# A convolution's buffer taken late, its norm run as a line of stages, and new counts of three engines' time in the order of a conformer layer

## The chip, the cores and the metric

The kernel runs on one core of one Trainium2 chip. The metric is the device time of one execution in microseconds (us); lower is better. The engines are named as in the profile: PE is TensorE (matmuls; PEld its weight loads), DVE is VectorE, ACT is ScalarE, POOL is GpSimd, and SP (SyncE) issues most of the DMAs.

## The reference

One inference step of a one-layer streaming encoder for a prompt of 2048 frames and a sample of 64, D_MODEL 1024, in float32. The two mixers work on the same normalised input, and the feed-forward part follows. Cut to what matters:

```python
h = rms_norm(x, p['norm1_g']) * (1 + sc1) + sh1
z = h @ p['w_in']
glu_a, glu_b, q, k, v, g_conv, g_attn = jnp.split(z, offs, axis=-1)

u = glu_a * jax.nn.sigmoid(glu_b)                       # (T, 512)
conv_out, conv_state = conv_module(u, conv_hist, ...)

q = rms_norm(q.reshape(B, T, 8, 64), p['q_norm_g'])
k = rms_norm(k.reshape(B, T, 8, 64), p['k_norm_g'])
o = attend(q, k, v, p['rel_bias'])                      # own chunk of 64 and the 8 before
attn_out = o @ p['w_attn_out']

merged = jax.nn.sigmoid(g_conv) * conv_out + jax.nn.sigmoid(g_attn) * attn_out
x = x + gt1 * (merged @ p['w_o'])
h2 = rms_norm(x, p['norm2_g']) * (1 + sc2) + sh2
gate, up = jnp.split(h2 @ p['w_ffn_in'], 2, axis=-1)
x = x + gt2 * ((jax.nn.silu(gate) * up) @ p['w_ffn_out'])

def conv_module(u, hist, w_dw, b_dw, ln_g, ln_b, w_out):
    ext = jnp.concatenate([hist, u], axis=1)
    y = depthwise_conv(ext, w_dw)                       # 31 taps, causal, 512 channels
    y = jax.nn.silu(layer_norm(y + b_dw, ln_g, ln_b))   # norm over the 512 channels
    return y @ w_out, ext[:, -30:]
```

The time is mostly matmuls with float32 operands that are split into a high and a low part (`hi` by ACT, `lo = x - hi` by DVE or POOL) and multiplied in three products.

## The kernel before

**Two phases.** The first phase goes over four blocks of tokens (576, then three of 512, the sample's 64 in the first): for each block the stages `q`, `0`, `k`, `1`, `v`, `2`, `3`, `g` of `ORDER`. `q`, `k`, `v` are projections; the stages 0 to 3 each make 128 channels (a column tile `ct`) of the convolution's input `u` by `glu`; `g` makes the 16 gate column tiles of both mixers. Beside these matmuls run the attention of the block, the taps of the convolution and its norm. The second phase takes three blocks of 576, 768 and 768 tokens: it merges both mixers (`merge`), applies `w_o`, and does the feed-forward part. Between the phases the first phase's pools are closed and the second's are opened in the same SBUF, so that a tile of the second phase waits for the last reader of what lay in its place.

**The order.** PE executes in the order in which the program emits its instructions. What accompanies the projections is written as generators in `Lane`s. A `Stream` holds a count of nanoseconds for each of `pe`, `dve`, `act` and `pool`; every instruction that goes through a `Meter` adds an estimate in `Stream.add` to its engine's count, beginning no earlier than PE's count. `stream.when("dve")` is DVE's count less 200 ns (`LAG`), and a generator that yields it is stepped on only when PE's count has come that far. Every 500 ns of PE's count `tick` looks at the lanes in the order norm_lane, work (q and k rows), attn, tail, conv. A lane may have a room: `conv` is stepped, up to four times a tick, only while DVE's count is less than 2000 ns ahead of PE's; attention may go to 3000 for DVE and 4000 for ACT. A yielded function parks the generator until it answers true. `drain` steps whatever is left, due or not. The estimates before: ACT 220 + 0.83 n ns for n elements of a partition, POOL 60 + 2.25 n (260 n for a power), DVE 75 + 1.04 n, or 0.75 n for `tensor_scalar` and copies and 8.3 n for a reciprocal. The other engines' order is made from the program by a scheduler; only PE's is as written.

**The convolution.** `convolve(u, y, ct, b)` multiplies the first of the 31 taps into `y[:, ct]` and adds 30 more, one DVE instruction each, `y <- u, wd, y`, with a yield after each. `u` has three buffers, `y` one for all four column tiles of a block. In stage 0 of each block the loop drains `conv` and `tail` and then takes a new `y`.

**The norm.** After stage 3 `conv_norm` goes to the lane `tail` (in block 0 twice, for the sample's 64 columns and the prompt's 512). It is parked until no convolution is open; then it sums the four column tiles on POOL (`s <- y`), adds up the channels by a matmul with ones (`pm`), subtracts the mean (DVE), squares (ACT), sums (POOL), a second matmul with ones, root (ACT), reciprocal (DVE, in four pieces), four products `y <- y, s` (POOL). Then for each column tile in turn: tanh (ACT, `ln <- y, lnh`), scale and product (DVE), high part (ACT, `part_h <- ln`), low part (DVE, `part_l <- ln, part_h`), and the store of both to `c_d` by SP, with a yield between each. `part_h` and `part_l` come from `parts()`, two buffers each, which the q and k rows (`store_kq`, from `kn`) and the attention's results (`finish_head`, from `o_p`) use as well.

**The end of the first phase.** At gate tile 10 of block 3 (`SIDE_G`) the loop drains `work` and `conv` and begins to load the second phase's first operands; after the last gate tile it drains `attn`, `conv` and `tail`.

Of the kernel before, what the change touches and what calls it, by code (L numbers as in the profile page):

```python
# [8 lines left out]
F32 = mybir.dt.float32  # L9
F32R = mybir.dt.float32r  # L10
AF = mybir.ActivationFunctionType
# [5 lines left out]
P = 128  # L17
# [7 lines left out]
TAPS = 31  # L25
# [149 lines left out]
class Stream:  # L175
# [7 lines left out]
    def add(self, name, op, n, args, kw):  # L183
        if name == "pe":
            x = args[1]
            if op == "transpose" or kw.get("is_transpose"):
                ns = 128 / 1.2
            elif x.dtype == F32:
                ns = max(n, 64) / (2.4 if "tile_position" in kw else 0.6)
            else:  # L190
                ns = (n if n >= 256 else 512) / 2.4
        elif name == "act":
            ns = 220 + 0.83 * n
        elif name == "pool":
            ns = 260.0 * n if ALU.pow in args else 60 + 2.25 * n
        else:
            fast = op in ("tensor_scalar", "tensor_copy")
            ns = 75 + n * (8.3 if op == "reciprocal" else 0.75 if fast else 1.04)
        self.load[name] = max(self.load[name], self.load["pe"]) + ns

    def full(self, room):
# [421 lines left out]
def streaming_layer(ctx: ExitStack, tc: tile.TileContext, I, O):  # L623
# [647 lines left out]
        W.done()  # L1271
        return u

    def convolve(u, y, ct, b):
        w = UW if b == 0 else HIST + QB
        n = w - HIST
        states = [(cs_s, HIST + SMP)] if b == 0 else [(cs_p, w)] if b == len(PBLOCKS) - 1 else []
# [2 lines left out]
        for rows_, e in states:  # L1280
# [4 lines left out]
            stream.at(stream.when("dve"), lambda s=s, rows_=rows_: nc.sync.dma_start(rows_[:, ct * P : (ct + 1) * P], s))  # L1285
            yield
        gps.tensor_copy(hist[:, ct], u[:, w - HIST : w])
        dve.tensor_scalar(y[:, ct, :n], u[:, :n], wd[:, ct, 0:1], bdw[:, ct : ct + 1], ALU.mult, ALU.add)
        for k in range(1, TAPS):
            with tc.issue_after(ahead_of_taps[-1]) if ahead_of_taps else nullcontext():  # L1290
                dve.scalar_tensor_tensor(
                    y[:, ct, :n], u[:, k : k + n], wd[:, ct, k : k + 1], y[:, ct, :n], ALU.mult, ALU.add
                )
            yield

    def conv_norm(y, c0, n, t0):
        yv = y[:, :, c0 : c0 + n]
        yield lambda: not conv.gens
        s = wk.tile([P, 512], F32, tag="ln_s", bufs=1)

        def total():
# [3 lines left out]

        gps.tensor_tensor(s[:, :n], yv[:, 0], yv[:, 1], ALU.add)
        for ct in (2, 3):
            gps.tensor_tensor(s[:, :n], s[:, :n], yv[:, ct], ALU.add)
        yield stream.when("pool") + PE_LAG
        pm = total()  # L1310
# [17 lines left out]
            dve.reciprocal(s[:, c:e], s[:, c:e])  # L1328
            yield
        yield stream.when("dve")  # L1330
        done = []
        for ct in range(4):
            gps.tensor_tensor(yv[:, ct], yv[:, ct], s[:, :n], ALU.mult)
            done.append(stream.when("pool"))
        for ct in range(4):
            yield done[ct]
            tmp = temp("ln")
            act.activation(tmp[:, :n], yv[:, ct], AF.Tanh, bias=lnh[:, 4 + ct : 5 + ct], scale=lnh[:, ct : ct + 1])
            yield stream.when("act")
            dve.tensor_scalar(yv[:, ct], yv[:, ct], lng[:, ct : ct + 1], lnb[:, ct : ct + 1], ALU.mult, ALU.add)  # L1340
            dve.scalar_tensor_tensor(tmp[:, :n], tmp[:, :n], 1.0, yv[:, ct], ALU.add, ALU.mult)
            yield stream.when("dve")
            hi, lo = parts()
            act.activation(hi[:, :n], tmp[:, :n], AF.Copy)
            yield stream.when("act")
            name = low(hi[:, :n], lo[:, :n], tmp[:, :n], n, TT_LESS)

            def store(ct=ct, hi=hi, lo=lo):
                for l, a in enumerate((hi, lo)):
                    nc.sync.dma_start(c_d[l, ct, :, t0 : t0 + n], a[:, :n].bitcast(F32))  # L1350

            stream.at(stream.when(name), store)

    def gates(b, free):

# [292 lines left out]
    for b, stage in ORDER:  # L1648
# [21 lines left out]
        elif stage == "g":  # L1670
            spare["open"] = b >= 2
            for g in gates(b, free):
# [7 lines left out]
                        norm_lane.add(gen)  # L1680
                if g == SIDE_G and b == len(PBLOCKS) - 1:
                    work.drain()
                    conv.drain()
                    while spare["heads"] and now["scored"] < spare["heads"][-1]:
                        attn.push()
                    stream.flush()
                    side.close()
                    wc = ctx.enter_context(tc.tile_pool(name="wc", bufs=1, side="right"))
                    cs = tile_chunks(*CBLOCKS[0])[0]
                    src = load_mixed(*cs, 0)  # L1690
                    first_gates = gate_columns(*cs, 0)
            norms = ahead
        else:
            if b == 0 and stage == 1:
                bias_rows()
            if stage == 0:
                conv.drain()
                tail.drain()
                y = wk.tile([P, 4, YW], F32, tag="y", name="y")
            conv.add(convolve(glu(b, stage), y, stage, b))  # L1700
            if stage == 3:
                if b == 0:
                    tail.add(conv_norm(y, 0, SMP, 0))
                    tail.add(conv_norm(y, SMP + HIST, QB, SMP))
                else:
                    tail.add(conv_norm(y, 0, QB, lo))
        for _ in range(MODS.get((b, stage), 0)):
            next(mods)
    next(mods)
    attn.drain()  # L1710
    conv.drain()
    tail.drain()
    stream.flush()
    side.close()
# [667 lines left out]
```

## Time and profile before

| what | before |
|---|---|
| median of 3 runs | 2942.79 us (2941.39 to 2945.29) |
| the profiled execution: its own time | 2941.67 us |
| its span, first to last instruction | 2939.5 us |
| busy: PE, DVE, ACT, POOL | 98%, 70%, 46%, 40% |
| mean granted clock of PE | 0.997 |
| HBM read and written | 476.53 and 148.54 MB |

The span is that of one profiled execution. A busy PE is not one at its peak: matmuls are pipelined and their ends modelled. "A <- B: x, n, m" in the list of waits means that A waited x us for B in total, n times, at most m us. "L105" is the line of `Meter` through which nearly all instructions are issued, so groups are told apart by the names of their tiles: out <- in. Phase one lasts until about 1163 us of the span; the four blocks' stage `q` ends at about 67, 341, 642 and 916 us.

### The profile page before, as it was taken

The page shows a single profiled execution, that of the slowest core. Times are in us where ns is not written, and L with a number is a line of the kernel's source. Part 1 is how long each engine was busy: PE and PEld are TensorE (multiplying, and loading weights), DVE is VectorE, ACT ScalarE, POOL GpSimd, SP SyncE. Part 2 cuts the span into 40 slices and gives each one's busy share as a digit, 9 for nine tenths or more (in the row PEclk, how much of TensorE's full clock was granted, in tenths as well). Part 3 has the DMA queues.
Part 4 walks back from the last instruction along what each step waited for, and adds up shares of the span by engine and source line. Part 5 has one row for each costly group of instructions (what it writes and reads, how often), then busy time and mean ns, then how long its engine had stood idle before and what let it go on. Part 6 is the DMA issues. An engine that isn't in the chain of part 4 may idle for free.

```text
span 2939.5 us, 44832 instructions
## 1 busy us (share of the span) xinstructions
PE 2889.3 (98%) x16193; PEld 2587.5 (88%) x16193; DVE 2053.9 (70%) x3648; ACT 1362.7 (46%) x2453; POOL 1164.9 (40%) x753
## 2 busy tenths in 40 slices
PE   7999999999999999999999999999999999999999
PEld 5899777888888887988999998999999999999998
DVE  5897788668967885577777756666666557566666
ACT  3346543751564266563444345444444345444442
POOL 1201210111011002553566452366567742465667
PEclk9999999999999999999999999999999999999999
DMA  9989899978996987984444875332333965333333
GB/s 322 315 305 314 287 281 329 285 232 306 285 297 197 320 270 224 291 295 157 144 144 146 292 261 200 97 122 94 115 115 104 346 220 179 97 103 106 115 107 127
DMA packets 467067, 628.04 MB, mean 214 GB/s; under 512 B 36196, under 2 KB 314584, under 8 KB 466845
## 3 DMA queue, kind: packets, MB, share of 16 engines
q1 hardware_dynamic: 452944, 606.11, 63.4%
q10 hardware_dynamic: 13901, 19.08, 1.9%
q8 instruction: 127, 2.08, 0.3%
q14 instruction: 95, 0.78, 0.1%
HBM read 476.53 MB, written 148.54 MB: 213 GB/s over the span
## 4 chain that ended last, share of the span: by engine, by line
PE 47%; DVE 2%; ACT 1%; DMA 1%; issue 1%; POOL 0%; SPq 0%; ACTq 0%; DVEq 0%; POOLq 0%
PE ps L105 29%; PE pd L105 13%; PE pw L105 5%; DVE wlo L105 1%; ACT whi L105 1%; DVE ps L105 0%; DMA cin<-o_d 0%; DMA x<-x_d 0%; DVE acc L105 0%; ACT xn L105 0%; DMA wst<-in_w_ffn_in 0%; DMA wfo<-in_w_ffn_out 0%; DMA tg<-g_d 0%; DVE sums L105 0%; PE pt L105 0%
## 5 line engine op out<-in xcount | busy, mean ns | idle before, releaser
L105 PE MATMUL ps<-t,whi 128*128 128x384 f32 (+1 forms) x2112 | 502.0, 322 | 2.8 <-ACT u L105 1.7
L105 POOL TENSOR_TENSOR wlo<-wst,whi 128x1024 fp32r<-128x1024 f32 (+1 forms) x159 | 362.7, 2293 | 246.1 <-ACT whi L105 214.4
L105 ACT ACTIVATE whi<-wst 128x1024 fp32r<-128x1024 f32 (+1 forms) x265 | 258.3, 979 | 316.1 <-PE ps L105 129.6
L105 PE MATMUL ps<-b,whi 128*128 128x384 f32 (+1 forms) x1584 | 380.7, 325 | 6.4 <-DVE v L105 2.1
L105 PEld LDWEIGHTS ps<-t,whi 128*128 128x128 f32 x2112 | 367.8, 188 | 10.1 <-ACT u L105 3.9
L105 DVE SCALAR_TENSOR_TENSOR y<-u,wd,y 128x512 f32<-128x512 f32 (+1 forms) x480 | 370.1, 774 | 8.0
L105 PE MATMUL ps<-hh,whi 128*128 128x512 f32 (+2 forms) x992 | 362.8, 366 | 0.1
L105 DVE TENSOR_TENSOR acc<-acc,pd 128x512 f32<-128x512 f32 x482 | 322.2, 685 | 48.1 <-PE pd L105 45.6
L105 PE MATMUL ps<-hh,wlo 128*128 128x512 f32 (+2 forms) x992 | 345.2, 348 | 0.0
L105 PE MATMUL ps<-hl,whi 128*128 128x512 f32 (+2 forms) x992 | 344.5, 347 | 0.0
L105 PE MATMUL ps<-t,wlo 128*128 128x384 f32 (+1 forms) x1056 | 338.5, 321 | 0.0
L105 PE MATMUL pd<-whi,hid 128*128 128x512 f32 x912 | 297.9, 391 | 0.6 <-DVE hid L105 0.3
L105 PEld LDWEIGHTS ps<-b,whi 128*128 128x128 f32 x1584 | 276.9, 188 | 14.6 <-DVE v L105 3.2
L105 ACT ACTIVATE pr<-pr,sm 128x640 f32<-128x640 f32 (+3 forms) x272 | 201.9, 749 | 137.1 <-DVE sm L105 134.8
L105 PE MATMUL ps<-b,wlo 128*128 128x384 f32 (+1 forms) x792 | 256.1, 323 | 0.0
L105 POOL TENSOR_TENSOR r<-t,mhalf 128x1 f32<-128x1 f32 (+2 forms) x68 | 82.3, 1219 | 403.7 <-DVE t L105 377.8
L105 PEld LDWEIGHTS ps<-hh,wlo 128*128 128x128 f32 x992 | 186.5, 188 | 22.6
L105 DVE TENSOR_TENSOR wlo<-wst,whi 128x1024 fp32r<-128x1024 f32 (+1 forms) x106 | 135.9, 1286 | 100.3 <-ACT whi L105 98.9
L105 PEld LDWEIGHTS pd<-whi,hid 128*128 128x128 f32 x912 | 171.2, 188 | 37.2 <-DVE acc L105 1.8
L105 PEld LDWEIGHTS ps<-hh,whi 128*128 128x128 f32 x992 | 187.0, 189 | 18.2 <-issue 3.3
L105 PEld LDWEIGHTS ps<-hl,whi 128*128 128x128 f32 x992 | 187.4, 189 | 14.3 <-issue 1.7
L105 PEld LDWEIGHTS ps<-t,wlo 128*128 128x128 f32 x1056 | 198.2, 188 | 0.8
(233 smaller groups left out, 6309.6 us busy)
## 6 DMA issues: line engine op xcount, KB each, us to landing
whi<-w_din_h SPq DMA_DIRECT2D x72, 512.0 KB, 6.4
wlo<-w_din_l SPq DMA_DIRECT2D x72, 512.0 KB, 7.3
wst<-sum_d SPq DMA_DIRECT2D x131, 256.0 KB, 3.1
wfo<-in_w_ffn_out SPq DMA_DIRECT2D x64, 512.0 KB, 4.1
wmod<-in_w_ada SPq DMA_DIRECT2D x46, 512.0 KB, 8.8
sum_d<-ws SPq DMA_DIRECT2D x88, 256.0 KB, 2.0
wst<-in_w_ffn_in SPq DMA_DIRECT2D x85, 256.0 KB, 3.2
wst<-in_w_in SPq DMA_DIRECT2D x40, 512.0 KB, 6.0
```

What stands on the lines that cost most here:

```text
L105: self.last = f(*args, **kw)
```

## The change

Three things change. (1) `Stream.add` counts ACT, POOL and DVE by other formulas; PE's stay. (2) `convolve` takes the buffer `y` itself, in column tile 0, after it has been parked until the norms of all blocks before are done; stage 0 of a block no longer drains `conv` and `tail`; instead every stage 0 to 3 lets at most two convolutions stay open before it adds the next (`drain_taps(2)`), and the two other drains of `conv` become `drain_taps(0)`, which steps the norm where a convolution is parked. (3) `conv_norm` begins when the first two column tiles have their taps, adds the third and the fourth when theirs are done, and its last part is a line of seven steps over the four column tiles: in step i it gives tile i-3 to the split and the store, does the DVE's part for i-2, the tanh for i-1 and POOL's product for i, with one yield between steps, for the latest of ACT, DVE and POOL.

```diff
--- before.py
+++ after.py
@@ -190,12 +190,17 @@
             else:
                 ns = (n if n >= 256 else 512) / 2.4
         elif name == "act":
-            ns = 220 + 0.83 * n
+            ns = 30 + 0.93 * n + (190 if kw.get("accum_out") is not None else 0)
         elif name == "pool":
-            ns = 260.0 * n if ALU.pow in args else 60 + 2.25 * n
+            ns = 300.0 + 230.0 * n if ALU.pow in args else 60 + 2.3 * n
         else:
             fast = op in ("tensor_scalar", "tensor_copy")
-            ns = 75 + n * (8.3 if op == "reciprocal" else 0.75 if fast else 1.04)
+            if op == "reciprocal":
+                ns = 95 + 5.9 * n
+            elif fast:
+                ns = 250 + 0.4 * n if n > 64 else 100
+            else:
+                ns = 75 + 1.04 * n + (60 if op == "scalar_tensor_tensor" and n > 64 else 0)
         self.load[name] = max(self.load[name], self.load["pe"]) + ns
 
     def full(self, room):
@@ -1271,7 +1276,9 @@
         W.done()
         return u
 
-    def convolve(u, y, ct, b):
+    ys, done = {}, {"taps": 0, "norms": 0}
+
+    def convolve(u, ct, b):
         w = UW if b == 0 else HIST + QB
         n = w - HIST
         states = [(cs_s, HIST + SMP)] if b == 0 else [(cs_p, w)] if b == len(PBLOCKS) - 1 else []
@@ -1285,17 +1292,31 @@
             stream.at(stream.when("dve"), lambda s=s, rows_=rows_: nc.sync.dma_start(rows_[:, ct * P : (ct + 1) * P], s))
             yield
         gps.tensor_copy(hist[:, ct], u[:, w - HIST : w])
+        yield lambda: done["norms"] == b
+        if not ct:
+            ys[b] = wk.tile([P, 4, YW], F32, tag="y", name="y")
+        y = ys[b]
         dve.tensor_scalar(y[:, ct, :n], u[:, :n], wd[:, ct, 0:1], bdw[:, ct : ct + 1], ALU.mult, ALU.add)
         for k in range(1, TAPS):
             with tc.issue_after(ahead_of_taps[-1]) if ahead_of_taps else nullcontext():
                 dve.scalar_tensor_tensor(
                     y[:, ct, :n], u[:, k : k + n], wd[:, ct, k : k + 1], y[:, ct, :n], ALU.mult, ALU.add
                 )
-            yield
-
-    def conv_norm(y, c0, n, t0):
-        yv = y[:, :, c0 : c0 + n]
-        yield lambda: not conv.gens
+            if k < TAPS - 1:
+                yield
+        done["taps"] += 1
+        yield
+
+    def drain_taps(left):
+
+        while len(conv.gens) > left:
+            while conv.parked(conv.gens[0]):
+                tail.step(tail.gens[0])
+            conv.step(conv.gens[0])
+
+    def conv_norm(b, c0, n, t0, last):
+        yield lambda: done["taps"] >= 4 * b + 2
+        yv = ys[b][:, :, c0 : c0 + n]
         s = wk.tile([P, 512], F32, tag="ln_s", bufs=1)
 
         def total():
@@ -1305,6 +1326,7 @@
 
         gps.tensor_tensor(s[:, :n], yv[:, 0], yv[:, 1], ALU.add)
         for ct in (2, 3):
+            yield lambda: done["taps"] >= 4 * b + ct + 1
             gps.tensor_tensor(s[:, :n], s[:, :n], yv[:, ct], ALU.add)
         yield stream.when("pool") + PE_LAG
         pm = total()
@@ -1328,28 +1350,39 @@
             dve.reciprocal(s[:, c:e], s[:, c:e])
             yield
         yield stream.when("dve")
-        done = []
-        for ct in range(4):
+        tmps = [None] * 4
+
+        def over(ct):
             gps.tensor_tensor(yv[:, ct], yv[:, ct], s[:, :n], ALU.mult)
-            done.append(stream.when("pool"))
-        for ct in range(4):
-            yield done[ct]
-            tmp = temp("ln")
-            act.activation(tmp[:, :n], yv[:, ct], AF.Tanh, bias=lnh[:, 4 + ct : 5 + ct], scale=lnh[:, ct : ct + 1])
-            yield stream.when("act")
+
+        def swish(ct):
+            tmps[ct] = temp("ln")
+            act.activation(tmps[ct][:, :n], yv[:, ct], AF.Tanh, bias=lnh[:, 4 + ct : 5 + ct], scale=lnh[:, ct : ct + 1])
+
+        def times(ct):
+            tmp = tmps[ct]
             dve.tensor_scalar(yv[:, ct], yv[:, ct], lng[:, ct : ct + 1], lnb[:, ct : ct + 1], ALU.mult, ALU.add)
             dve.scalar_tensor_tensor(tmp[:, :n], tmp[:, :n], 1.0, yv[:, ct], ALU.add, ALU.mult)
-            yield stream.when("dve")
+
+        def give(ct):
+            tmp = tmps[ct]
             hi, lo = parts()
             act.activation(hi[:, :n], tmp[:, :n], AF.Copy)
-            yield stream.when("act")
             name = low(hi[:, :n], lo[:, :n], tmp[:, :n], n, TT_LESS)
 
-            def store(ct=ct, hi=hi, lo=lo):
+            def store():
                 for l, a in enumerate((hi, lo)):
                     nc.sync.dma_start(c_d[l, ct, :, t0 : t0 + n], a[:, :n].bitcast(F32))
 
             stream.at(stream.when(name), store)
+
+        for i in range(7):
+            for step, ct in ((give, i - 3), (times, i - 2), (swish, i - 1), (over, i)):
+                if 0 <= ct < 4:
+                    step(ct)
+            if i < 6:
+                yield stream.when("act", "dve", "pool")
+        done["norms"] += last
 
     def gates(b, free):
 
@@ -1680,7 +1713,7 @@
                         norm_lane.add(gen)
                 if g == SIDE_G and b == len(PBLOCKS) - 1:
                     work.drain()
-                    conv.drain()
+                    drain_taps(0)
                     while spare["heads"] and now["scored"] < spare["heads"][-1]:
                         attn.push()
                     stream.flush()
@@ -1693,22 +1726,19 @@
         else:
             if b == 0 and stage == 1:
                 bias_rows()
-            if stage == 0:
-                conv.drain()
-                tail.drain()
-                y = wk.tile([P, 4, YW], F32, tag="y", name="y")
-            conv.add(convolve(glu(b, stage), y, stage, b))
+            drain_taps(2)
+            conv.add(convolve(glu(b, stage), stage, b))
             if stage == 3:
                 if b == 0:
-                    tail.add(conv_norm(y, 0, SMP, 0))
-                    tail.add(conv_norm(y, SMP + HIST, QB, SMP))
+                    tail.add(conv_norm(b, 0, SMP, 0, False))
+                    tail.add(conv_norm(b, SMP + HIST, QB, SMP, True))
                 else:
-                    tail.add(conv_norm(y, 0, QB, lo))
+                    tail.add(conv_norm(b, 0, QB, lo, True))
         for _ in range(MODS.get((b, stage), 0)):
             next(mods)
     next(mods)
     attn.drain()
-    conv.drain()
+    drain_taps(0)
     tail.drain()
     stream.flush()
     side.close()
```

## The prediction

> **What bounds the kernel now.** I read the page first, then the list of waits, then stretches of time around the longest waits, and last the timelines of single engines there.
>
> ```profile
> PE 2889.3 (98%) x16193; PEld 2587.5 (88%) x16193; DVE 2053.9 (70%) x3648; ACT 1362.7 (46%) x2453; POOL 1164.9 (40%) x753
> ```
>
> TensorE (PE) is busy for 98% of the span, and it runs its instructions in the order in which the program wrote them. So the end moves by what PE loses between its matmuls, not by the load of another engine: VectorE (DVE) has 70%, ScalarE (ACT) 46%, GpSimd (POOL) 40%. The next question is who made PE wait.
>
> ```profile
> PE pa L105 <- DMA wmod<-in_w_ada: 6.4, 6, 3.4
> PE pt L105 <- DVE kn L105: 6.1, 2, 4.0
> PE ps L105 <- DVE t L105: 5.8, 5, 3.4
> ```
>
> These are the three largest releasers (total, number, longest). Behind kn and t stands one wait each of 4.0 and 3.4 us; the six of the DMA lie partly in the start. The stretches around them (columns: stretch, length, then busy time and count of PE, PEld, DVE, ACT, POOL, then PE's granted clock and DMA) show that a long wait is paid twice:
>
> ```profile
> 356.50:361.60 5.10, 1.14 (x8) 1.04 (x8) 2.40 (x4) 1.35 (x3) 0.00 (x0) 1.00 0.84 250
> 361.60:368.40 6.80, 6.80 (x23) 5.82 (x23) 4.71 (x11) 3.13 (x6) 0.00 (x0) 0.50 1.08 386
> 466.00:471.00 5.00, 2.58 (x27) 0.70 (x26) 3.68 (x8) 1.75 (x3) 0.67 (x1) 0.98 1.06 396
> 471.00:474.40 3.40, 3.21 (x15) 2.11 (x16) 0.42 (x1) 0.00 (x0) 0.00 (x0) 0.53 1.03 414
> 1171.60:1175.30 3.70, 0.28 (x3) 0.02 (x2) 1.29 (x3) 0.00 (x0) 0.22 (x1) 0.82 0.51 169
> 1174.00:1180.80 6.80, 5.51 (x21) 5.51 (x22) 3.43 (x8) 0.88 (x3) 0.00 (x0) 0.50 0.90 273
> ```
>
> In 1171.6 to 1175.3 PE did almost nothing, and from 1174.0 to 1180.8 its clock was granted at 0.50. In 356.5 to 361.6 it worked for 1.14 us, and until 368.4 it had half its clock again. The first costs 3.7 us, and half of the 5.5 us in which it then worked at half speed, 2.75: **6.4 us**, called C below. The second costs about 4.0, and half of 6.8, 3.4: **7.4 us**, called A. A third, B (466 to 474), costs 2.4 and half of 3.4, 1.7: 4.1 us; it waits for modulation weights. The page on the TensorE clock, "TensorE: Matmul & The Clock Gate" of the Trainium skill (Part 1: The HAM clock gate), says that about 3.4 us of sustained work bring the full rate back; by that C would be worth 5.4 us, A 5.7, and the forecast below 2937.5 instead of 2936. The trace disagrees for A and C, 6.8 us at half, and agrees for B's 3.4.
>
> **The change, part by part.**
>
> *The end of block 3's norm (C).* Who holds PE there:
>
> ```profile
> PE ps L105 <- DVE t L105: 3.4, 1, 3.4
> DVE t L105 <- DMA c_d<-part_l: 2.4, 1, 2.4
> ```
> ```profile
> 1165.86 0.68 DVE L105 TENSOR_TENSOR part_l<-o_p,part_h 128x512 fp32r<-128x512 f32 x1
> ...
> 1169.59 2.79 DVE L105 TENSOR_TENSOR part_l<-ln,part_h 128x512 fp32r<-128x512 f32 x1 [0.70 <-DMA o_d<-part_l]
> 1174.75 0.49 DVE L105 SCALAR_TENSOR_TENSOR t<-tg,ps 128x320 f32<-128x320 f32 x1 [2.38 <-DMA c_d<-part_l]
> ```
> ```profile
> 1172.40 0.32 SPq L1350 DMA_DIRECT2D c_d<-part_l  x1
> ```
>
> The merge of the second phase writes t where the first phase kept its split buffers (part_h, part_l). The norm of the last block writes the last of them at 1169.59, its store is issued at 1172.40, and only when that has been read does t run, at 1174.75; PE's banks fill up at 1171.6 meanwhile. So the question is when the norm's last part is made. Today:
>
> ```profile
> L105 DVE SCALAR_TENSOR_TENSOR y<-u,wd,y x480: 730/752/929, 85.5 to 1089.2; 128x512 f32<-128x512 f32 x120, 128x606 f32<-128x606 f32 x40
> ```
> ```profile
> L105 POOL TENSOR_TENSOR y<-y,s x4: 1090/1189/1307, 1126.9 to 1130.5; 128x512 f32<-128x512 f32 x4
> ```
> ```profile
> L105 ACT ACTIVATE ln<-y,lnh x4: 800/808/821, 1130.1 to 1163.8; 128x512 f32<-128x512 f32 x4
> ...
> L105 DVE TENSOR_TENSOR part_l<-ln,part_h x4: 666/684/2786, 1133.8 to 1169.6; 128x512 fp32r<-128x512 f32 x4
> ```
>
> (Durations are least/median/most in ns, then first and last start.) The last tap runs at 1089.2, the four products with 1/std start at 1126.9, and the four tanh are spread over 1130.1 to 1163.8: 33.7 us for three column tiles' distance, 11.2 us each, with four waits of the order in each, 2.8 us a wait. The rest is drained when attention is over. The new line has six waits in all: 6 x 2.8 = 17 us after 1126.9, and some 2 us for the last split, 1146. Each of its waits is for the latest of three engines, so up to 4 us: 1153. Against that the taps are counted dearer: 607 becomes 75 + 532 + 60 = 667 ns, and they are released against a bound on VectorE's count:
>
> ```profile
> L105 DVE SCALAR_TENSOR_TENSOR y<-u,wd,y 128x512 f32<-128x512 f32 x120 | 90.1, 751 | 2.5
> ```
>
> 120 x 60 ns = 7.2 us later if VectorE's count is what holds them, nothing if not. The norm then ends at 1146 to 1160. What is late next is the last attention head, whose part_l was written at 1165.86 and whose store freed its buffer by 1169.59 (the row above: the norm's last step starts right then). t would run at about 1169.8, its second step 0.5 us later, before PE's 1171.6. So C goes: **-6.4 us**, between 0 (norm still last) and -6.4.
>
> *The forced drain at block 1 (A).* Today the first column stage of a block emits all that is left of the last norm at once. In block 1 that is four of everything, from 341 on:
>
> ```profile
> PE pt L105 <- DVE kn L105: 4.0, 1, 4.0
> ...
> ACT part_h L105 <- DMA c_d<-part_h: 1.1, 1, 1.1
> ```
> ```profile
> L105 ACT ACTIVATE part_h<-ln x4: 613/624/633, 343.9 to 356.5; 128x512 fp32r<-128x512 f32 x4
> ...
> L105 ACT ACTIVATE part_h<-pt,gqk x3: 687/687/689, 335.8 to 362.5; 128x512 fp32r<-128x512 f32 x3
> ```
> ```profile
> 358.26 0.69 ACT L105 ACTIVATE part_h<-pt,gqk 128x512 fp32r<-128x512 f32 x1 [1.10 <-DMA c_d<-part_h]
> ```
> ```profile
> 359.02 0.75 DVE L105 SCALAR_TENSOR_TENSOR part_l<-pt,gqk,part_h 128x512 fp32r<-128x512 f32 x1 [1.13 <-ACT part_h L105]
> 359.68 0.68 DVE L105 TENSOR_TENSOR kn<-kn,r 128x512 f32<-128x512 f32 x1
> ```
>
> The split buffers are a ring of two. Four norm parts stand in it ahead of a q tile's part, which starts at 358.26 when a norm store has been read; VectorE runs its low half at 359.02, and behind that in its queue kn, at 359.68; PE needed kn at 356.5. The change takes the drain away: the norm goes on at its own pace, and only the taps, parked until it is done, wait for it. Its parts then go through the ring from about 335 on, a few us apart, instead of between 344 and 357; but they meet the same q tiles, whose parts fall due from 336 to 363. I take half: **-3.7 us**, bounds 0 and -7.4 (a wait shortened under some 3.5 us would lose its half-clock part whole). The parked taps cost nothing as long as block 1's taps have room:
>
> ```profile
> L105 DVE SCALAR_TENSOR_TENSOR y<-u,wd,y x120: 731/751/882, 364.5 to 519.7; 128x512 f32<-128x512 f32 x120
> ```
> ```profile
> L105 DVE TENSOR_SCALAR y<-u,wd,cols x2: 540/540/540, 660.9 to 698.2; 128x512 f32<-128x512 f32 x2
> ```
>
> Today they run from 364.5 to 519.7, and block 2 first needs their buffer at 661; a start 10 us later is hidden by those 141 us, in which the norm takes some 60. A parked tap is not yet in VectorE's queue, so nothing stands behind it. Keeping at most two convolutions open before a new one matches the three u buffers and emits taps that are due anyway: 0, with up to +1 us.
>
> *The counts.* No instruction is added or removed; the moments change at which PE's next matmuls are written into its order. ScalarE's 512 columns fall from 645 to 506 counted ns, an Exp of 640 with its sum rises from 751 to 815, VectorE's short products rise (128 columns: 171 to 301), GpSimd's change by 2%. PE's own count is left as it is, and it runs fast: 384 columns are counted 160 ns, while
>
> ```profile
> 1832.99 31.60 PE ps L105 x180
> ```
>
> is 175.6 ns a matmul, 1.10 times as long. So every due time is stretched by a tenth on the chip. For a split of probabilities the trace has
>
> ```profile
> L105 DVE TENSOR_TENSOR pl<-ptp,ph 128x512 fp32r<-128x512 f32 x128 | 87.4, 688 | 44.8 <-ACT ph L105 44.1
> ...
> L105 ACT ACTIVATE ph<-ptp 128x512 fp32r<-128x512 f32 x128 | 74.9, 590 | 57.5 <-PE ptp L105 57.2
> ```
>
> 590 + 688 = 1278 ns. Due with its two lags (400 - 200) it was after 645 + 607 + 200 = 1452, stretched 1597, and is now after 506 + 607 + 200 = 1313, stretched 1444. A reserve of 0.32 us shrinks to 0.17 where both engines are free; where they have work before it, VectorE's dearer taps push due times out instead. In between I take **+3 us** of short waits over both phases, bounds -3 and +20 (128 chunks x 0.139 x 1.10 = 19.6 if none had a reserve). In the second phase the same counts set the residual's transposes and GpSimd's share of the splits, with too few instances to move more than 1 or 2 us; in the +3.
>
> **Sum.** -6.4 - 3.7 + 3 = -7.1 us. The profiled execution took 2941.67 us, 2.2 more than its span, and lies 1.1 under the median of 2942.79; from the median the forecast is **2936 us**. A difference under 0.2% (5.9 us) can't be told from none here; the shown runs differ by 3.9.
>
> **Rivals.**
>
> 1. *The norm is still the last to end* (no change of C). Taps 7 us later, and each of the six waits as long as the rooms that attention may fill (4 us of ScalarE), plus the steps before the products, give 1160 to 1168: then the last parts are drained behind attention as today. For it: the rows of 1130 to 1163. Against: ten waits fewer. Time 2942.8 - 3.7 + 2 = 2941.
>
> 2. *ScalarE's counts, now without reserve, make PE wait in attention* (slower). Place: the products with V, written after ph and pl, all through the gate stages. Price 0.153 us a chunk, 19.6 for all 128; with C gone and A unchanged it decides for slower from (5.9 + 6.4) / 0.153 = 80 chunks on. At three quarters it gives 2942.8 + 14.7 - 6.4 = 2951. For it:
>
> ```profile
> PE po L105 <- DVE pl L105: 0.8, 3, 0.3
> ```
>
> Only 0.8 us of PE's waits are for pl today: the old counts were safe there and can only lose. Against: 0.17 us of reserve are left, and steps come only every 500 counted ns.
>
> 3. *GpSimd's products block VectorE.* The norm's last part took 2786 ns instead of 684, while GpSimd ran a split:
>
> ```profile
> 1169.43 2.39 POOL L105 TENSOR_TENSOR wlo<-wst,whi 128x1024 fp32r<-128x1024 f32 x1 [5.71 <-ACT whi L105]
> ```
>
> In the line, products of GpSimd run beside VectorE's two-input steps, twice in each of five norms: 10 x 2.1 = 21 us of VectorE at most. If a third reaches PE: 2936 + 7 = 2943. "SBUF — State Buffer" of the Trainium skill (Who interferes with whom) says that such an instruction with two SBUF inputs and one of GpSimd that reads SBUF exclude each other wholly. By that rule the trace agrees, 2786 ns against 684. Against the rival: VectorE has 30% free.
>
> **How the numbers follow.** The forecast's case has 0.52, and its own range is 2929 (A gone whole, no new waits) to 2941; 0.46 of it is faster by over 0.2%, 0.06 within. Rival 1 has 0.14, within. Rival 2 has 0.26, slower. Rival 3 has 0.08, half within, half slower. Faster 0.46, same 0.24, slower 0.30. The range reaches down to B gone as well, 2929 - 4 = 2925, and up over rival 2's value to 2953, leaving its worst part out.
>
> **What would show it.** C right: t no longer waits for c_d<-part_l, the norm's last part is made before the last o_p, and no stretch at clock 0.50 stands at the phases' border. A right: PE's wait for kn of 4.0 us shrinks, and with it the half clock after it. Counts right: PE's waits for pl and pr stay under 2 us together. Wrong: a new wait of PE over 3 us elsewhere, with its stretch at half clock; or many waits of 0.1 to 0.3 us for pl, sm and pr.

## The result and the profile after

The changed kernel takes **2966.91 us** (median of 4 runs, 2963.09 to 2971.61) against 2942.09 for the kernel before on the same chip (4 runs, 2940.19 to 2945.29): a ratio of 1.0086, 95% interval 1.0071 to 1.0100. It is slower by 0.86%, some 25 us; forecast were 2936, within 2925 to 2953. The profiled execution took 2968.08 us, its span 2966.3.

The page of the changed kernel, busy time and share of each engine:

```profile
PE 2893.4 (98%) x16193; PEld 2591.5 (87%) x16193; DVE 2041.3 (69%) x3635; ACT 1363.7 (46%) x2453; POOL 1185.9 (40%) x766
```

TensorE's work is the same 16193 matmuls; 4.1 us more of busy time stand against 26.8 us more of span. So most of it is time in which PE did nothing, or ran at half clock after a wait (its mean granted clock fell from 0.997 to 0.992). Thirteen splits of weights moved from VectorE (3648 instructions before) to GpSimd (753 before), since the counts also choose the engine of a split; they lie for the most part in the second phase, which did not get longer. The list of waits of PE (total us, number, longest):

```profile
PE sc L105 <- DVE sm L105: 12.1, 4, 6.1
PE sc L105 <- DMA kk<-k_d: 7.2, 2, 5.1
PE pt L105 <- DVE x_t L105: 5.2, 3, 3.6
...
PE po L105 <- DVE pl L105: 3.6, 2, 3.0
PE pm L105 <- POOL s L105: 2.7, 2, 2.0
```

Before, sc waited 2.7 us for sm, and the list had no row for kk or pm. The single waits for kn (4.0 us) and t (3.4 us), on which the forecast rests, are gone. The two largest new ones lie in block 1, while attention of block 0 runs beside it. Their stretches (length, busy time and count of PE, PEld, DVE, ACT, POOL, PE's clock, DMA share and GB/s):

```profile
383.00:389.60 6.60, 6.60 (x32) 5.21 (x32) 6.50 (x10) 2.59 (x5) 0.83 (x1) 1.00 0.92 318
389.60:396.20 6.60, 0.49 (x3) 0.05 (x2) 1.06 (x7) 0.27 (x2) 1.64 (x1) 0.87 1.09 316
396.20:406.40 10.20, 10.20 (x33) 8.61 (x34) 8.25 (x20) 4.86 (x14) 0.00 (x0) 0.58 0.28 91
497.70:503.00 5.30, 0.43 (x2) 0.00 (x0) 1.37 (x3) 0.00 (x0) 0.00 (x0) 0.75 0.78 186
503.00:509.80 6.80, 6.53 (x26) 5.62 (x27) 2.25 (x5) 1.41 (x3) 0.00 (x0) 0.69 0.72 209
```

PE had 0.49 us of work in the 6.6 us of the second row, and ran the next 10.2 us at a mean clock of 0.58; then 0.43 us of work in 5.3 us, and 6.8 us at 0.69. What it waited for is seen on two other engines' timelines (start, us, engine, operation, and in brackets the idle time before it and its releaser; a row with x2 or x4 takes several instructions together, with what the queue stood between them). SyncE's queue:

```profile
381.20 0.33 SPq L1375 DMA_DIRECT2D c_d<-part_h  x1
...
383.38 0.38 SPq L484 DMA_DIRECT2D wlo<-w_din_l  x1
383.86 2.30 SPq L254 DMA_DIRECT2D wmod<-in_w_ada  x4
386.21 1.16 SPq L1506 DMA_DIRECT2D bias<-rb_d  x2
387.48 0.60 SPq L1462 DMA_DIRECT2D kk<-q_d  x1
388.19 0.65 SPq L1463 DMA_DIRECT2D kk<-k_d  x1
...
391.38 0.45 SPq L1463 DMA_DIRECT2D kk<-k_d  x1
```

VectorE:

```profile
390.37 0.22 DVE L105 TENSOR_TENSOR pl<-ptp,ph 64x64 fp32r<-64x64 f32 x1 [0.28 <-ACT ph L105]
395.81 0.29 DVE L105 CUSTOM_DVE_ANT_0 pr<-sc,bias 128x128 f32<-128x128 f32 x1 [5.22 <-DMA bias<-rb_d]
```

and PE, at the end of the chain:

```profile
396.17 0.80 PE L105 MATMUL sc<-kk,q 128*128 128x256 f32 x2 [6.11 <-DVE sm L105]
```

Four modulation slabs (wmod, 512 KB each) are issued at 383.86, and the bias of the next head 2.3 us later, directly behind them. DMA is full (share 0.92 and 1.09 in the two stretches above). VectorE's pr stood 5.22 us for the bias, so its sm came at 396, and PE's next scores stood 6.11 us for a bank. The order grants a bias at least 6000 counted ns (BIAS_LAG) from the moment at which its load is written into the program. Ahead of these loads SyncE had stood for a split part of the norm (one of its waits from 374 to 397):

```profile
SPq L1375 <- ACT part_h L105: 4.2, 1, 4.2
```

In the kernel before, the same two groups of transfers lie 16 us apart:

```profile
362.89 2.37 SPq L249 DMA_DIRECT2D wmod<-in_w_ada  x4
...
378.66 1.19 SPq L1473 DMA_DIRECT2D bias<-rb_d  x2
```

In the second place the loads of q and k stand behind four slabs:

```profile
483.61 4.05 SPq L254 DMA_DIRECT2D wmod<-in_w_ada  x4
488.56 0.61 SPq L1462 DMA_DIRECT2D q<-q_d  x1
...
492.44 0.44 SPq L1463 DMA_DIRECT2D kk<-k_d  x1
493.84 10.00 SPq L1506 DMA_DIRECT2D bias<-rb_d  x2
```

Here sc waited 5.14 us for k_d. The row of 10.00 us is two issues of about 0.45 us each; between them SyncE stood, by the profile for an earlier transfer (its waits from 488 to 505):

```profile
SPq L1506 <- DMA g_d<-gate: 9.1, 1, 9.1
```

I call this **the collision**: no instruction was added; two groups of loads that had missed each other now meet, and the readers are ready before the later group lands. The meeting alone isn't enough. In e2 below, the changed kernel with the old counts, the same bias is issued 2.4 us behind the same four slabs:

```profile
368.17 2.27 SPq L249 DMA_DIRECT2D wmod<-in_w_ada  x4
370.60 1.71 SPq L1501 DMA_DIRECT2D bias<-rb_d  x2
```
```profile
384.39 0.27 DVE L105 CUSTOM_DVE_ANT_0 pr<-sc,bias 128x128 f32<-128x128 f32 x1
```

There pr ran 13.8 us after the issue and did not wait. In the changed kernel VectorE was ready for it at 390.59, 4.4 us after the issue.

### The profile page after: what moved, and what is told of

Read it like the earlier page. It is cut to its first block, busy times and chain, and to the rows that moved or that the text cites. A ratio compares the mean times of both kernels' runs of the same rounds, so it can differ in the third digit from the quotient of the medians.

```text
span 2966.3 us, 44835 instructions
## 1 busy us (share of the span) xinstructions
PE 2893.4 (98%) x16193; PEld 2591.5 (87%) x16193; DVE 2041.3 (69%) x3635; ACT 1363.7 (46%) x2453; POOL 1185.9 (40%) x766
## 4 chain that ended last, share of the span: by engine, by line
PE 48%; DVE 2%; ACT 1%; DMA 1%; issue 1%; POOL 0%; ACTq 0%; POOLq 0%; DVEq 0%; SPq 0%
PE ps L105 29%; PE pd L105 14%; PE pw L105 5%; DVE wlo L105 1%; ACT whi L105 1%; DVE ps L105 0%; DMA cin<-o_d 0%; ACT xn L105 0%; DMA wfo<-in_w_ffn_out 0%; POOL wlo L105 0%; DMA wst<-in_w_ffn_in 0%; DVE acc L105 0%; DMA tg<-g_d 0%; DVE sums L105 0%; PE pt L105 0%
## 5 line engine op out<-in xcount | busy, mean ns | idle before, releaser
L105 POOL TENSOR_TENSOR wlo<-wst,whi 128x1024 fp32r<-128x1024 f32 (+1 forms) x166 | 375.9, 2276 | 258.8 <-ACT whi L105 243.7
L105 POOL TENSOR_TENSOR r<-t,mhalf 128x8 f32<-128x8 f32 (+2 forms) x68 | 85.4, 1264 | 414.8 <-DVE t L105 396.4
L105 POOL TENSOR_TENSOR wlo<-ws,whi 128x512 fp32r<-128x512 f32 x100 | 131.6, 1335 | 166.4 <-ACT whi L105 166.4
```

The costliest lines, as they stand in the source:

```text
L105: self.last = f(*args, **kw)
```

## The experiments

The theories, as the expectations name them. K: the loss is the counts' own price, at whatever structure. S: it is that of the norm's new structure. D: it is the collision, loads that come too late because the moments moved. E, put against D later: the new moments hurt in general and the loads only coincide. X and Y are told where they come.

Ratios are to the kernel before on the same chip, with 95% intervals. Stage lengths run from the first projection matmul of a block to the first of the next, the second phase from its first matmul to the end of the last; they are of the one profiled execution of each kernel.

### The parts alone

e1: the kernel before with the counts of the change. e2: the changed kernel with the old counts.

```diff
 e1 (on before.py)
-            ns = 220 + 0.83 * n
+            ns = 30 + 0.93 * n + (190 if kw.get("accum_out") is not None else 0)
 ... (and VectorE's and GpSimd's)
 e2 (on after.py): the same lines the other way
```

> The kernel before with the new counts alone; convolution and norm as before. Theory K (the counts move attention's loads and matmuls against the engines and the DMA queue, and that is the loss): 2960 to 2972, with PE's long waits for sc behind a late bias or k load in 270 to 530 us, as in the changed kernel. Theory S (the late buffer, the parked taps and the line are the loss): 2938 to 2948, no wait of PE for sc over 2 us.

> The changed kernel with the old counts. Theory K: 2930 to 2942, with the wait at the phases' border gone. Theory S: 2960 to 2970. If both parts only perturb an order that was fitted to the old one, each of the two kernels lies some 10 to 15 us over the kernel before.

e1 took 2948.55 us, 1.0017 [1.0002, 1.0031], with runs from 2940.59 to 2962.77; e2 2944.69 us, 0.9998 [0.9989, 1.0008]. e3 has the line of stages alone, e4 the late buffer alone (old norm), both with the old counts:

```diff
 e3 (on before.py): conv_norm's end only
-        for ct in range(4):
-            yield done[ct]
 ...
+        for i in range(7):
+            for step, ct in ((give, i - 3), (times, i - 2), (swish, i - 1), (over, i)):
 e4 (on after.py): conv_norm's end and the counts as before
```

> The kernel before with the norm's last part as a line of seven steps, with its buffer, drains, parking and counts as before. Theory K: 2933 to 2943; if the border's wait C goes, as predicted, some 6 us under the kernel before. Theory S, if the line is the part of it that costs: 2950 or more, with waits for parts of the split's ring.

> The changed kernel with the old counts and the norm's last part as before, column tile after column tile: only the late buffer, the parked taps, the limit of two open convolutions and the norm's earlier begin are left. Theory K: 2936 to 2946. Theory S, if the parked taps cost: 2955 or more, with VectorE late for kn, x_t or sm in blocks 0 and 1.

e3: 2947.58 us, 1.0019 [1.0010, 1.0028]. e4: 2941.04 us, 0.9988 [0.9979, 0.9998], the fastest version with all its loads, and that by 0.1%, less than can be told apart with safety. Of the four expectations only e4's under theory K (2936 to 2946) was met. So the counts alone cost some 5 us, the structure alone nothing, and both together 25; the line alone costs some 4. Neither K nor S holds. The stages of the profiled executions show two things in block 1:

```
stage (us)              before   e4      e3      e2           e1        after
                                 buffer  line    structure    counts
block 1, q and column 0   44.9    46.1    48.7    49.7         50.8      55.0
block 1, rest            252.2   248.3   246.7   245.6        248.9     261.9
```

In the first of them the parts nearly add up: the structure 4.9 us (of which the late buffer 1.2), the counts 5.9, both 10.2. In the rest every part alone is shorter than before, and only both together are longer. One more row speaks against a simple story: e4 has a wait for kk of the second kind, and is fast all the same.

```profile
PE sc L105 <- DMA kk<-k_d: 6.7, 3, 4.1
```

### Half of the counts

```diff
 e7 (on after.py)
-            ns = 30 + 0.93 * n + (190 if kw.get("accum_out") is not None else 0)
+            ns = 220 + 0.83 * n
 e8 (on after.py): VectorE's lines back, ScalarE's and GpSimd's kept
```

> The changed kernel with ScalarE's old count alone. If ScalarE's lower count makes the difference (rival 2 of the prediction): 2938 to 2948. If VectorE's: it stays at 2958 to 2970. Theory D, in which any shift can bring the loads together, expects no rule: between both.

> The changed kernel with VectorE's old counts alone. If VectorE's dearer taps make the difference (the taps of block 3 end at 1127.7 us instead of 1089.2): 2938 to 2948. If ScalarE's count does: 2958 to 2970. Theory D: between both, with the waits for sc where a bias load follows modulation loads by less than some 10 us.

2957.32 us, 1.0048 [1.0032, 1.0064], and 2957.23 us, 1.0047 [1.0030, 1.0064]. Either half back recovers some 10 us (9.6 and 9.7 of the 22.2 us that lie between the medians of the changed kernel and e2). So neither ScalarE's counts, the forecast's second rival, nor VectorE's are the culprit by themselves. Theory D expected a result between both, and so would two costs that simply add up: these runs don't tell the two apart. In both, block 1's first stage keeps its length (56.9 and 56.3 us), and the rest of block 1 falls to 248.3 and 253.2.

### Moving the modulation's steps

The steps that load those slabs stand one in each of block 1's and block 2's four column stages. e5 and e6 put two in each of block 2's, none in block 1, in the changed kernel and in the kernel before:

```diff
-MODS = {(b, ct): 1 for b in (1, 2) for ct in range(4)}
+MODS = {(2, ct): 2 for ct in range(4)}
```

> The changed kernel with the second modulation's eight steps all in block 2, two a stage, so that none of their 512 KB loads are issued in block 1, where PE waited 6.3 and 5.3 us for attention's scores at 390 and 498 us. Theory D (attention's bias and k loads were issued right behind four such loads, and came late): those two waits go, 2945 to 2956. Theory E (the engines are late by themselves, the loads happen to end last): the waits stay, 2960 to 2970.

> The same move in the kernel before, as the control of the run beside it. Theory D: no wait of that kind is there to remove, only the short waits for the modulation's own loads at 467 to 472 (4 us with the half clock) move: 2936 to 2946. If the move helps both kernels by the same amount, it tells nothing of the collision.

2992.49 us, 1.0168 [1.0151, 1.0184], and 2983.09 us, 1.0131 [1.0116, 1.0146]: both much slower, since block 2 cannot take the loads. The waits of PE, e5:

```profile
PE pa L105 <- DMA wmod<-in_w_ada: 32.8, 18, 9.8
```

Both expected totals were missed because of that. The question itself is answered by block 1 behind its first stage: 261.9 us become 230.9 in the changed kernel (-31.0), 252.2 become 238.2 in the kernel before (-14.0). Of that, 9 and 11 us are work of PE (its busy time times its granted clock) that moved out with the modulation's steps. The loads cost the changed kernel 17 us more there, and without them it is the shorter one by 7. The waits at 396 and 503 are gone.

### Leaving the loads out

A cleaner cut: no slab is loaded from block 1 on, the modulation's steps multiply the slabs already held, so the output is no longer the layer's.

```diff
+            if len(self.ready) >= 20:
+                self.ready.append(self.ready[-4])
+                continue
             (src,), a, b = self.source(self.keys[len(self.ready)])
```

> The changed kernel without the modulation's loads from block 1 on: the modulation's steps multiply the slabs that are there already (other numbers, the same instructions), so 28 loads of 512 KB are left out. Theory D: the waits at 390 and 498 go and those for wmod too, 2945 to 2950 us, and level with the next kernel or below it by the border's 3 to 6 us. Theory E: stays above 2957, some 20 us over the next kernel.

> The control: the kernel before with the same 28 loads left out. Both theories: only the wait for wmod at 466 with its half clock (4.1 us) goes, 2936 to 2940 us.

e10: 2950.51 us, 1.0030 [1.0018, 1.0043]. e11: 2938.43 us, 0.9983 [0.9973, 0.9992]. Leaving the loads out saves 2966.9 - 2950.5 = 16.4 us in the changed kernel and 2943.8 - 2938.4 = 5.4 us in the kernel before: **the collision is some 11 us of the 25**, with an uncertainty of 6 us, as it is a difference of three ratios with the intervals above. The first place shows why. In e10 SyncE stood for the norm's part as well, but no slabs follow, and the bias came in time:

```profile
381.85 1.11 SPq L1509 DMA_DIRECT2D bias<-rb_d  x2
```
```profile
388.04 0.28 DVE L105 CUSTOM_DVE_ANT_0 pr<-sc,bias 128x128 f32<-128x128 f32 x1
```

pr ran 6.2 us behind the issue without a wait, instead of 9.6. The remaining 12 us are seen by stages of these two:

```
stage (us)              before   after   e11 (before,   e10 (after,
                                          no loads)      no loads)
block 0                  310.7   315.9      311.6          312.0
block 1, q and column 0   44.9    55.0       44.2           57.0
block 1, rest            252.2   261.9      247.6          239.9
block 2                  273.5   277.9      273.5          277.8
block 3                  283.3   283.1      285.3          283.8
second phase            1769.8  1767.1     1768.9         1768.6
```

e10 against e11: +12.8 in block 1's first stage, -7.7 in its rest, +4.3 in block 2, all else within 1.5. Without the collision block 1's rest is shorter than before, and a second loss stands ahead of it. Theory D had expected e10 level with e11 or below, theory E some 20 us above; it is 12 above, so both miss, and E, that the new moments hurt in general, has its share too.

The work that PE does in block 1's two parts differs by some 2 us between these kernels. What it loses there (the stage's length less PE's busy time times its granted clock, an estimate from the traces) in block 1's first stage is 0.9 us before, 9.1 in the changed kernel, 0.7 in e11 and 11.3 in e10; in the rest 13.1, 23.6, 9.0 and 1.6. Block 0's 5.2 us are no part of either account: 4.7 of them lie in its stage `q` (which ends at 67.0 us before, 71.7 after), and that end lies between 67.0 and 72.3 in all profiled executions; what moves it stays open.

### Allowances

Can the order buy the collision off? e9 grants attention's loads 5 us more, e12 frees the slabs' loads 10 us of PE's count later:

```diff
 e9
-QK_LAG = 9000.0
+QK_LAG = 14000.0
-BIAS_LAG = 6000.0
+BIAS_LAG = 11000.0
 e12
-        self.stream.at(self.stream.when("pe"), lambda n=self.given: self.free(n), True)
+        self.stream.at(self.stream.when("pe") + (10000.0 if self.given > 16 else 0.0), lambda n=self.given: self.free(n), True)
```

> The changed kernel with BIAS_LAG 6000 -> 11000 and QK_LAG 9000 -> 14000: the order grants attention's loads 5 us more of PE's count before it writes the scores; nothing else changes. Theory D (the loss is loads that land later than the order grants, behind the modulation's 2 MB): TensorE's waits sc<-sm at 390 (6.1 us) and sc<-kk at 498 (5.1 us) and the half clock behind them go, 2945 to 2955 us. Theory E (the moments at which matmuls are written are spoiled in general by the new counts, the loads only coincide): other waits take their place, 2960 us or more.

> The changed kernel with each modulation load from block 1 on freed to start 10 us of PE's count later; the same loads and the same work. Theory D: in block 1 attention's k and bias go ahead of the slabs, both sc waits go, the slabs still have some 30 us before their use, 2945 to 2955 us, if the slabs don't meet the next head's loads. Theory E: 2960 us or more.

2963.79 us, 1.0071 [1.0056, 1.0086], and 2964.02 us, 1.0074 [1.0059, 1.0089]. Theory D's expectations missed on both totals, and E's (2960 us or more) were met. The two waits at 396 and 503 did go, in both runs. In e9 block 1's rest fell to 229.0 us, but 15.5 us of PE's work (busy time times granted clock, 222.8 us instead of 238.3) had only moved out of it; block 2 grew to 304.1, with a wait of 5.30 us for kk at 671, and block 3 to 292.4. In e12 the rest fell by 9.3 us, with 8.7 us of waits for wmod in eight places in the list. A wait removed by a later due time came back elsewhere.

### Block 1's first stage

In the changed kernel PE waits there for a row tile of the norm, and 28 us later for attention:

```profile
327.94 0.66 PE L105 MATMUL pt<-ident,x_t 128*128 128x128 f32 x4 [3.55 <-DVE x_t L105]
...
355.76 0.51 PE L105 MATMUL sc<-kk,q 128*128 128x256 f32 x2 [2.78 <-DVE sm L105]
```

With the half clock behind the second (0.50 for 3.4 us from 357.0 on, 1.7 us lost) these are 8.0 of the 8.2 us that PE loses there more than before. The load of x_t was issued at 319.69:

```profile
319.69 1.17 SPq L1161 DMA_DIRECT2D x_t<-in_x_prompt  x1
```

Theory X held that this load is late for its allowance. e13 grants it 5 us more; e14 does so without the modulation's loads:

```diff
-X_LAG = 8000.0
+X_LAG = 13000.0
```

> The changed kernel with X_LAG 8000 -> 13000: the order grants the load of a norm's rows 5 us more. Theory X (the 8 to 10 us lost in block 1's q stage are the third row tile, loaded at 319.7 and wanted by TensorE 4.6 us later): the wait pt<-x_t at 324 with its half clock goes, the q stage and its convolution column fall from 55 us to about 47, 2958 us. Rival Y (the stage is late because ScalarE and VectorE are, with the norm of block 0 beside it): another wait of the same stage takes its place, 2964 us or more.

> The changed kernel without the modulation's loads from block 1 on (as in the tenth run) and with X_LAG 13000. If the two kinds of late loads are the whole loss beside block 2's 4 us: 2940 to 2944 us, level with the kernel before without the same loads (2938) within 5 us. If something else holds block 1's q stage: 2948 us or more.

2966.28 us, 1.0076 [1.0061, 1.0091], and 2949.05 us, 1.0019 [1.0010, 1.0029]. Theory X falls and Y stands: the wait for x_t went, the stage kept its 55.6 and 56.1 us, because another wait took its place. PE of e13:

```profile
327.32 0.79 PE L105 MATMUL ps<-wlo,hh 128*128 128x512 f32 x1 [4.87 <-POOL wlo L105]
```

GpSimd of e13:

```profile
321.61 3.37 POOL L105 TENSOR_TENSOR y<-y,s 128x512 f32<-128x512 f32 x3 [9.43 <-DVE sm L105]
324.93 2.34 POOL L105 TENSOR_TENSOR wlo<-wst,whi 128x1024 fp32r<-128x1024 f32 x1
```

GpSimd made three products of block 0's norm, 3.37 us, ahead of a split of weights (wlo) for which PE stood 4.87 us. In the kernel before, that split ran at 309.98, before the stage began:

```profile
309.98 2.41 POOL L105 TENSOR_TENSOR wlo<-wst,whi 128x1024 fp32r<-128x1024 f32 x1 [14.68 <-ACT whi L105]
```

In the changed kernel it runs at 318.69, in e13 at 324.93. So the stage is short of more than one thing: a row tile, a weight split, the norm's products. Which step would have to move first wasn't settled. In e13 the collision's two waits also shrank, from 6.11 and 5.14 us to 3.04 and 1.56, though no load of attention was given more time.

### Allowances with the old counts

e15: the structure with the old counts and X_LAG 11000. e16: the late buffer with the old counts and QK_LAG 12000.

```diff
 e15                      e16
-X_LAG = 8000.0          -QK_LAG = 9000.0
+X_LAG = 11000.0         +QK_LAG = 12000.0
```

> The structure of the change with the old counts (2944.7 us) and X_LAG 8000 -> 11000. Theory X: its three waits for x_t, 4.4 us, go with their half clock, 2938 to 2942 us, perhaps better than both kernels. Rival Y: 2943 to 2948.

> The late buffer alone with the old counts and the old norm (2941.0 us) and QK_LAG 9000 -> 12000. Its waits sc<-kk are 6.7 us. If a later due time covers them: 2934 to 2938 us, below both kernels. If the later scores push work to the block's end, as with both allowances of attention raised in the changed kernel: 2941 to 2950.

2953.41 us, 1.0031 [1.0020, 1.0043], and 2954.04 us, 1.0032 [1.0021, 1.0042]: both slower than without the edit (2944.69 and 2941.04), and outside every range that was expected. One constant of 3 us, meant to remove 4 to 7 us of waits, cost 9 to 13.

## Why the prediction was wrong

**The border of the phases (C): right in its mechanism, worth less.** The norm's tanh, in the changed kernel:

```profile
L105 ACT ACTIVATE ln<-y,lnh x4: 802/811/817, 1155.6 to 1174.8; 128x512 f32<-128x512 f32 x4
```

Four column tiles now take 19.2 us instead of 33.7. Read from the border (the second phase's first matmul, 1193.8 here and 1164.6 before), not from the span's start:

```profile
1179.37 3.70 DVE L105 TENSOR_TENSOR part_l<-ln,part_h 128x512 fp32r<-128x512 f32 x2 [2.48 <-ACT part_h L105]
...
1192.34 0.69 DVE L105 TENSOR_TENSOR part_l<-o_p,part_h 128x512 fp32r<-128x512 f32 x1 [0.70 <-ACT part_h L105]
...
1198.81 0.49 DVE L105 SCALAR_TENSOR_TENSOR t<-tg,ps 128x320 f32<-128x320 f32 x1 [5.46 <-DMA wst<-in_w_o]
```

The norm's last part lies at 1180.2 to 1183 and ends 11 us ahead of the border; before, it began 5 us behind it. The last head's is at 1192.3, and t waits no longer for c_d (the profile names weights, wst). The second phase is 4.6 us shorter in e3, 4.1 in e2, 2.7 here, and in e10 against e11 only 0.3, where 6.4 were forecast. Other waits take part of the gain: in e10 PE waits 2.3 us for t and 1.3 for a gate around the border.

**The drain in block 1 (A): the gain is there without the loads, its mechanism isn't shown.** The wait for kn of 4.0 us is gone, but it is gone in e1 and e3 too, and both keep the drain. Without the slabs' loads block 1's rest is 7.7 us shorter, about the 7.4 of the far bound and not the half that I took; with them and the old counts (e2) it is 6.6 shorter. In the changed kernel itself it is 9.7 us longer, since the collision lies in the same stages.

**The counts (+3, bounds -3 and +20): this step failed.** On the new structure they cost some 22 us (2966.91 against e2's 2944.69, on another chip; by the two ratios to the kernel before 26), alone 5.3. I priced them as reserves between pairs of engine operations, 0.139 us a chunk. No such price was seen: of the 3.6 us of waits for pl, 3.0 are one wait, at 1161, with another cause (below). What moved was when whole transfers were issued on SyncE's queue, and when their readers came. Counts of compute engines decide when a step is written, and with it when its loads are issued; the sum had no term for that, though the trace of before showed slabs and head loads on the same queue. What the runs show in the term's place is the collision, some 11 us, and block 1's first stage.

In that stage the sum had nothing but "0, with up to +1 us" for the parked taps and two open convolutions. That term itself was about right: the late buffer alone (e4) makes the stage 1.2 us longer. The line alone adds 3.9 (e3) and the counts alone 5.9 (e1), and the sum had no term for either in that stage.

The forecast's own signs said the same: PE's waits for pl and pr were to stay under 2 us and are 3.8, and the new waits over 3 us with a stretch at half clock, its sign of being wrong, are the 6.11 and 5.14 us of block 1.

**Rival 2** gives the right side with the wrong mechanism: taking ScalarE's counts back recovers 9.6 us (e7), but no more than VectorE's do (e8), and the products with V don't decide. **Rival 3** came true in one place. During the products of the line, VectorE:

```profile
1156.43 1.70 DVE L105 TENSOR_SCALAR y<-y,cols 128x512 f32<-128x512 f32 x1 [0.80 <-ACT ln L105]
1158.05 1.58 DVE L105 TENSOR_TENSOR part_l<-o_p,part_h 128x512 fp32r<-128x512 f32 x1
...
1162.07 0.69 DVE L105 TENSOR_SCALAR y<-y,cols 128x512 f32<-128x512 f32 x1
```

and GpSimd and PE:

```profile
1154.24 4.83 POOL L105 TENSOR_TENSOR y<-y,s 128x512 f32<-128x512 f32 x4 [13.51 <-DVE s L105]
```
```profile
1161.01 0.50 PE L105 MATMUL po<-pl,vv 128*128 128x512 f32 x1 [3.01 <-DVE pl L105]
```

A product with constants, whose median is 0.54 us, took 1.70, and a split, whose median is 0.69, took 1.58, beside GpSimd's 4.83 us of products, and PE stood 3.01 us for pl. "SBUF — State Buffer" of the Trainium skill (Who interferes with whom) says that two-input work of VectorE excludes GpSimd's reads, and that tensor_scalar can do so too in its two-port mode; both rows agree. e2 has the same line and no such wait, so the line does not bring it by itself, and its 3.01 us and the half clock behind it (3.4 us at 0.50) are smaller than the two losses above. **Rival 1** fell.

In sum, by the profiles of e10 and e11: 12.8 - 7.7 + 4.3 + 0.4 - 1.5 - 0.3 = 8.0 us, as much as their spans differ, and the collision's 11 us on top. The medians of e10 and e11 differ by 12.1: the profiled execution of e10, 2945.85 us, was the fastest of its six. Not settled: what holds block 2 (+4.3; one new wait there, pm for s of 2.0 us, is a part), and what in block 1's first stage would have to move.

Single executions differ, too: the kernel before spread over 12 us in 31 runs (2938.26 to 2950.19), e1 over 22 in ten, of which a single execution makes half. That transfers which just meet make this spread was not tried.

## What to carry to other kernels

In a kernel whose order is written from counted times, a change of counts is a change of every transfer's moment: before costing it, list which loads of each queue are issued within a few microseconds of a group of large ones, how long after the issue their reader comes, and what stands in the queue ahead of them. An allowance for a load is only good for the traffic that it was set in, and raising it moved the loss (e9, e13, e15, e16) instead of removing it. Better counts are not a better order: the constants around them had been set against the old ones, and here each part alone cost some 5 us at most while the sum cost 25.

## What the hardware showed

- Two small loads behind 2 MB on one queue: the bias issued at 386.21 released VectorE at 395.81, 9.6 us later; without the 2 MB (e10) its reader ran 6.2 us after the issue and had not waited for it.
- SyncE's queue goes on in order: at 493.84 the second of two bias loads, with an issue of 0.45 us, was issued 9.1 us behind the first, and all loads behind it with it.
- The clock's price for an idle stretch isn't fixed. Granted in the changed kernel:

```profile
394.50:404.70 10.20, 8.53 (x26) 7.23 (x27) 7.00 (x16) 4.00 (x10) 0.00 (x0) 0.50 0.39 107
500.30:507.10 6.80, 3.83 (x12) 3.28 (x13) 0.00 (x0) 0.00 (x0) 0.00 (x0) 0.50 0.54 152
357.00:360.40 3.40, 3.40 (x11) 2.54 (x12) 2.81 (x8) 1.30 (x5) 0.33 (x1) 0.50 1.08 356
```

Half clock lasted 10.2 us from within the wait of 6.11 us on, 6.8 us from within that of 5.14 us on, and 3.4 us behind one of 2.78 us. The prediction took it that a wait under some 3.5 us would cost no half clock; the last row shows one that did.
